# Neighbourhood attention in strips of 16 rows by 8 columns, in a one-core diffusion trunk step

## The chip, the cores and the metric

The kernel runs on one core of one Trainium2 chip. The metric is device microseconds from start to end of one execution; the median of several executions counts. All arithmetic is in 32-bit floats. TensorE (PE) multiplies, VectorE (DVE), ScalarE (ACT) and GpSimd (POOL) do the elementwise work, and all data transfers are issued from SyncE's queue (SP).

## The reference, cut to what matters

One layer of a trunk works on 1024 latent tokens (a grid of 16 rows by 64 columns) and 256 context tokens, each 1024 wide: SwiGLU, then four mixers side by side (A to D, 256 channels each), an output projection, and a second SwiGLU. Mixer C, with 4 heads of 64, is the one that matters here. A latent query sees a window of 8 rows by 16 columns of its grid, clamped at the edges, with a learned bias per offset, and besides all 256 cached context keys, in one softmax:

```python
rs = jnp.clip(rows - wr // 2, 0, R - wr)             # wr = 8, R = 16
row_idx = rs[:, None] + jnp.arange(wr)[None, :]
cs = jnp.clip(cols - NAT_WC // 2, 0, GRID_W - NAT_WC)  # NAT_WC = 16, GRID_W = 64
in_win = (cols[None, :] >= cs[:, None]) & (cols[None, :] < cs[:, None] + NAT_WC)
s_loc = jnp.where(in_win, einsum(q, k[row_idx]) * scale + bias, NEG_INF)
s_ctx = einsum(q, k_ctx) * scale
p = softmax(concatenate([s_loc, s_ctx]))
o = p_loc @ v[row_idx] + p_ctx @ v_ctx
```

## The kernel before, in words

The program is written down in a natural order and recorded by a planner (`Plan`, lines 213 to 413). The planner finds what each instruction needs from earlier ones, and issues them as a list schedule: each engine takes, of the instructions whose inputs are there by the planner's prices (`price`, line 425), the one written first. Nearly every instruction is therefore issued from line 395, and groups in the profile are told apart by tile names. To decide what overlaps, `View.box` (line 139) takes the smallest range that holds a view; for a tensor in DRAM that is a range of addresses from its first to its last element.

The order of the stages is: first SwiGLU, projections and mixers A and D, projection of B, then attention. Attention runs over units, each a tile of 128 queries of one pair of heads: 16 units of mixer B on all latent keys (`Gqa`), 4 of B's context, then for each of the two head pairs of C eight `Nat` units (line 1441) and two `Ctx` units. While unit n's second half (`back`) is written down, unit n+1's first half (`front`) and the query load of unit n+2 (`prep`, `load_q`, line 1222) precede it. Probabilities have 4 buffers, that is two units.

A `Nat` unit holds two grid rows by 64 columns of queries (128). Its keys are all columns of 8 or 9 grid rows (`KR0`, line 28; `nrow` is 9 for units 2 to 5): 512 or 576 local keys, and 256 context keys. For each of two heads, `front` multiplies queries and keys in two products each (the query's high and low part): 512 columns, 64 more where there are 9 rows, 256 context columns. DVE adds the bias and takes the maximum (`tensor_tensor_reduce`, lines 1471 to 1475), ACT takes the exponentials with their sums, and `softmax_tail` (line 1305) multiplies by the reciprocal of the sum; for the second head that is done on POOL where n is 832. `back` calls `pv` (line 1251): TensorE transposes the probabilities in blocks of 128 keys (6 blocks, and one of 64), the first four are copied to SBUF by ACT, the rest by DVE, and each is multiplied with its values; then `split` writes the result as a high part (ACT) and a low part (DVE) into `yh` and `yl`, the input of the output projection.

The projections of C (`c_tasks`, line 1140) are worked by token tile. They store normalised queries and keys (512 columns, `craw`) and values (256, `cvraw`) into a DRAM tensor `csc` [10 tiles, 128 tokens, 768], one transfer for each; the first three tiles before attention, the other tiles as side work between units of B. `CSet` (line 1349) then loads a head pair's keys (`load_k`), values and the bias tables (`bint` 576 columns, `bedge` 896 columns per head). Side work during C is loading the second pair's set, splitting the other mixers' outputs (`y_piece`), and a part of the output projection (`wo_early`, tile `fb`) from unit 5 of the second pair on, which has lower priority and fills TensorE.

Of the kernel before, what the change touches and what calls it, by code (L numbers as in the profile page):

```python
# [27 lines left out]
KR0 = [0, 0, 0, 2, 4, 6, 8, 8]  # L28
# [26 lines left out]
class View:  # L55
    """a part of a planned tile: offset and (size, stride) per dimension, and how to take it from the tile"""
# [156 lines left out]
class Plan:  # L213
# [28 lines left out]
    def record(self, eng, real, meth, a, k):  # L242
# [44 lines left out]
    # -- the list schedule, and the issue in its order --  # L287
# [137 lines left out]
def price(eng, meth, a, k):  # L425
    """about how long an engine is held, in microseconds"""
# [48 lines left out]
def write_down(plan, I, O):  # L475
# [85 lines left out]
    def mod_section_dve(s, f):  # L561
        """128 columns of section s: sum over the features on VectorE"""
# [18 lines left out]
    def mod_tile(ws):  # L581
        """silu(c) times two [1024, 128] tiles of weights: [128 columns, tile, vector]"""
# [14 lines left out]
    def mod_first(f):  # L597
        """128 columns of the first shift and scale"""
# [74 lines left out]
    def gemm_fm(ps, whi, wlo, hh, hl, c, ks=range(KT), first=0, last=KT - 1):  # L673
        """feature-major: ps[128, chunk] = w[:, 128 cols]^T h"""
# [89 lines left out]
    def first(c, fetch, wab, js):  # L764
        """the first block: its products follow the loads of the modulation's weights"""
# [55 lines left out]
    def tables():  # L821
# [17 lines left out]
        # retention tables  # L839
# [37 lines left out]
    # ================= mixers =================  # L877
# [137 lines left out]
    def d_process(p):  # L1015
        """heads 2p and 2p + 1: states of both directions, block-diagonal over the heads; then the tiles' outputs"""
# [122 lines left out]

    def c_tasks(bank, early):  # L1140
        """the projections of C by token tile, for an accumulator of one bank"""
        wts = []

        def qk_tile(t):
# [9 lines left out]
            dma(csc[t][:, 0:512], raw)  # L1154
# [3 lines left out]
        def v_tile(t):  # L1158
# [7 lines left out]
            dma(csc[t][:, 512:768], raw[:, 0:256])  # L1166
# [41 lines left out]
    # ================= attention =================  # L1208
# [13 lines left out]
    def load_q(src, t, pr):  # L1222
        """token-major heads 2pr, 2pr+1 -> [128, 2, 2, 128]: [hi; lo] and [lo; hi] per head"""
# [20 lines left out]
    def PYB(w):  # L1244
        """w columns of the outputs' bank; its groups come one after another"""
        if pyo[0] + w > 512:
            pyo[0] = 0
        pyo[0] += w
        return pyb[:, pyo[0] - w:pyo[0]]

    def pv(pr, t, probs, vtiles):
        """probs[e]: [128 q, nkeys]; vtiles(e): list of (key offset, n keys, v ap [n, 64])"""
        c, o = tok_chunk(t)
# [28 lines left out]
        split(yh[c][:, fi, o:o + P], yl[c][:, fi, o:o + P], py)  # L1282
# [22 lines left out]
    def softmax_tail(probs, sums, n):  # L1305
# [3 lines left out]
        for e in range(2):  # L1309
            (G if e and n == 832 else V).tensor_scalar(probs[e][:, :n], probs[e][:, :n], rs[:, e:e + 1], None, ALU.mult)  # L1310
# [4 lines left out]
    def load_k(src, col, lat, cxt, t0, n, wide=False):  # L1315
        """keys of token tiles, token-major [128, 2 heads, 64] -> [hi; lo] x 128 tokens per tile and head"""
# [33 lines left out]
    class CSet:  # L1350
        """a head pair of C: keys, values and bias"""

        def __init__(self, pr, q):
# [5 lines left out]
            self.bint = q.tile([P, 2, 576], F32, name="bint")  # L1359
            self.bedge = q.tile([P, 2, 896], F32, name="bedge")  # L1360
# [18 lines left out]
    class Ctx:  # L1379
        """context queries on context keys"""  # L1380
# [60 lines left out]
    class Nat:  # L1441
        def __init__(self, pr, i):
            self.pr, self.i = pr, i
            self.kr0 = KR0[i]
            self.nrow = 9 if 2 <= i <= 5 else 8
# [4 lines left out]
        def front(self):  # L1450
            pr, i, qT, kr0, nrow = self.pr, self.i, self.qT, self.kr0, self.nrow
            s_ = sets[pr]
            nk = 64 * nrow
            n = nk + 256
            probs = self.probs = new_probs()
            mx = ap.tile([P, 2, 3], F32, name="mx", tag="mx")
            nm = ap.tile([P, 2], F32, name="nmc", tag="nmc")
            sums = ap.tile([P, 2, 2], F32, name="sums3", tag="sums3")
            r9 = nk - 512
            for e in range(2):  # L1460
                sa, sb = PS2(), PS2()
                qk(sa, qT, e, s_.k[e][:, kr0 * 64:kr0 * 64 + 512])
# [310 lines left out]
```

## Time and profile before

| | us |
|---|---|
| median of 3 runs | 2652.24 |
| fastest, slowest run | 2649.84, 2653.35 |
| span of the profiled execution, first to last instruction | 2647.6 |
| TensorE busy | 2604.6 |
| VectorE, ScalarE, GpSimd busy | 1338.2, 740.4, 199.4 |
| TensorE's share of the chain that ended last | 93% |

The page gives the profiled execution by its span only, with no time of its own beside it; the span is 4.6 us below the median of the runs. Busy time is a union of the instructions of an engine; TensorE's matmuls are pipelined and their ends are modelled, so its busy time counts the tails of its products as busy. The chain of waits takes each instruction from where the one before it on the chain ended, and so shows what TensorE spends per product when products follow one another.

### The profile page before, as it was taken

To read this page: it belongs to the slowest core of one execution; us is meant where nothing else is said; L and a number is where in the kernel's file an instruction comes from. 1 tells how busy PE (TensorE), PEld (TensorE's weight loads), DVE (VectorE), ACT (ScalarE), POOL (GpSimd) and SP (SyncE) were. 2 spreads that over 40 slices of the span, in tenths; PEclk is the share of its full clock that TensorE was granted. 3 is DMA by queue.
4 is the path that set the end of the run, shared out by engine and by line. 5 is a ranking of instruction groups with operands and counts; after the bars stand their busy time and mean duration, and the time that the engine had idled before them with its cause. 6 is when DMAs were issued, how large, how long until landed. Compare 5 with 4: busy or idle time off the path is not lost.

```text
span 2647.6 us, 36536 instructions
## 1 busy us (share of the span) xinstructions
PE 2604.6 (98%) x14960; PEld 2192.8 (83%) x14960; DVE 1338.2 (51%) x2653; ACT 740.4 (28%) x1417; POOL 199.4 (8%) x243
## 2 busy tenths in 40 slices
PE   7999999999999999999999999999999999999999
PEld 5888888888888878887778678888888888888888
DVE  6755666554342374477665784354343233433433
ACT  5211111111111165322674783341111111111111
POOL 0000000000000041122100251220000000000000
PEclk9999999999999999999999999999999999999999
DMA  8322222222011131341301423011111111110112
GB/s 298 111 87 84 92 84 78 94 80 64 33 32 48 33 113 66 112 126 57 101 29 41 139 76 120 25 44 53 33 40 40 33 48 32 40 41 32 48 33 88
DMA packets 92119, 187.12 MB, mean 71 GB/s; under 512 B 9904, under 2 KB 39600, under 8 KB 91824
## 3 DMA queue, kind: packets, MB, share of 16 engines
q1 hardware_dynamic: 91952, 184.80, 21.1%
q8 instruction: 117, 1.92, 0.3%
q14 instruction: 50, 0.41, 0.0%
HBM read 156.97 MB, written 27.79 MB: 70 GB/s over the span
## 4 chain that ended last, share of the span: by engine, by line
PE 93%; DVE 5%; ACT 1%; issue 1%; DMA 1%; SPq 0%; POOL 0%; ACTq 0%; DVEq 0%; POOLq 0%
PE po L395 23%; PE pa L395 22%; PE pb L395 22%; PE pgd L395 3%; PE fb L395 3%; PE ptb L395 3%; PE pwo L395 3%; PE pyb L395 3%; PE ps L395 3%; PE p L395 1%; PE pd L395 1%; DVE nt L395 1%; DVE hl L395 1%; DVE dst L395 1%; PE pgate L395 1%; PE dpa L395 1%
## 5 line engine op out<-in xcount | busy, mean ns | idle before, releaser
L395 PE MATMUL po<-uh,whi 128*128 128x512 f32 (+1 forms) x1056 | 376.3, 356 | 4.3 <-DVE x L395 4.3
L395 PE MATMUL po<-ul,whi 128*128 128x512 f32 (+1 forms) x1056 | 375.7, 356 | 0.0
L395 PE MATMUL po<-uh,wlo 128*128 128x512 f32 (+1 forms) x1056 | 375.4, 356 | 0.0
L395 ACT CAST whi<-raw 128x1024 fp32r<-128x1024 f32 x162 | 168.5, 1049 | 715.7 <-PE po L395 487.7
L395 PE MATMUL pa<-hh,whi 128*128 128x512 f32 (+1 forms) x1024 | 363.5, 355 | 0.0
L395 PE MATMUL pb<-hh,whi 128*128 128x512 f32 (+1 forms) x1024 | 362.9, 354 | 0.0
L395 PE MATMUL pa<-hh,wlo 128*128 128x512 f32 (+1 forms) x1024 | 361.7, 353 | 0.0
L395 PE MATMUL pb<-hh,wlo 128*128 128x512 f32 (+1 forms) x1024 | 361.6, 353 | 0.0
L395 PE MATMUL pa<-hl,whi 128*128 128x512 f32 (+1 forms) x1024 | 359.9, 351 | 0.1
L395 PE MATMUL pb<-hl,whi 128*128 128x512 f32 (+1 forms) x1024 | 359.6, 351 | 0.0
L395 DVE TENSOR_TENSOR silu<-silu,pb 128x256 f32<-128x256 f32 (+1 forms) x128 | 76.2, 596 | 522.1 <-PE pb L395 522.1
L395 DVE TENSOR_TENSOR wlo<-raw,whi 128x1024 fp32r<-128x1024 f32 x162 | 198.3, 1229 | 181.4 <-ACT whi L395 179.1
L395 DVE SCALAR_TENSOR_TENSOR xr<-po,modT,xr 128x512 f32<-128x512 f32 (+1 forms) x264 | 174.1, 662 | 110.9 <-PE po L395 110.7
L395 PEld LDWEIGHTS po<-uh,whi 128*128 128x128 f32 x1056 | 198.6, 188 | 37.6 <-DVE x L395 5.1
L395 PEld LDWEIGHTS po<-ul,whi 128*128 128x128 f32 x1056 | 198.8, 188 | 32.5
L395 PEld LDWEIGHTS po<-uh,wlo 128*128 128x128 f32 x1056 | 198.7, 188 | 32.5
L395 PEld LDWEIGHTS pa<-hh,wlo 128*128 128x128 f32 x1024 | 192.1, 188 | 29.5
L395 PEld LDWEIGHTS pb<-hh,wlo 128*128 128x128 f32 x1024 | 192.0, 187 | 29.5
L395 PEld LDWEIGHTS pa<-hl,whi 128*128 128x128 f32 x1024 | 192.2, 188 | 28.6 <-DVE hl L395 0.5
L395 PEld LDWEIGHTS pb<-hl,whi 128*128 128x128 f32 x1024 | 192.2, 188 | 28.3 <-issue 0.2
L395 PEld LDWEIGHTS pa<-hh,whi 128*128 128x128 f32 x1024 | 192.4, 188 | 26.0 <-issue 0.4
L395 ACT CAST uh<-silu 128x512 fp32r<-128x512 f32 x132 | 72.2, 548 | 506.8 <-DVE silu L395 506.8
(446 smaller groups left out, 3969.7 us busy)
## 6 DMA issues: line engine op xcount, KB each, us to landing
raw<-in_w SPq DMA_DIRECT2D x132, 512.0 KB, 3.6
wh<-in_wmodT SPq DMA_DIRECT2D x96, 256.0 KB, 2.6
wmt<-in_wmod SPq DMA_DIRECT2D x20, 512.0 KB, 6.9
raw<-in_wfm SPq DMA_DIRECT2D x10, 512.0 KB, 3.5
xr<-xs SPq DMA_DIRECT2D x8, 640.0 KB, 6.5
x<-in_xT SPq DMA_DIRECT2D x16, 256.0 KB, 5.5
xs<-x SPq DMA_DIRECT2D x16, 256.0 KB, 2.0
raw<-in_wo SPq DMA_DIRECT2D x8, 512.0 KB, 3.5
```

The source lines that it names most:

```text
L395: getattr(real, meth)(*[f(v) for v in a], **{q: f(v) for q, v in k.items()})
```

## The change

Units of C are cut from the grid in the other direction. A `Nat` unit is now a strip of all 16 grid rows by 8 columns (128 queries again, so 8 units per head pair), and its keys are its own strip and the one on either side: 384 local keys for units 1 to 6, 256 for units 0 and 7. The window's rows are now part of the mask, which the host writes into the bias tables. The tokens are put into strip order when the projections are stored to `csc`, by two transfers of 64 tokens per tile in place of one; results go back to token order in `pv`, by two strided splits of 64 columns. The context scores of both heads share one bank (`PS1`) and one maximum; the second head's multiplication goes to POOL where n is 640.

```diff
+    def to_strips(t, col, src):
+        n = src.shape[1]
+        if t >= 8:
+            dma(csc[t][:, col:col + n], src)
+            return
+        for rr in range(2):
+            r = 2 * t + rr
+            dma(csc[0:8, 8 * r:8 * r + 8, col:col + n], src[64 * rr:64 * rr + 64])
...
-            dma(csc[t][:, 0:512], raw)
+            to_strips(t, 0, raw)
...
-            dma(csc[t][:, 512:768], raw[:, 0:256])
+            to_strips(t, 512, raw[:, 0:256])
...
     def pv(pr, t, probs, vtiles):
...
-        split(yh[c][:, fi, o:o + P], yl[c][:, fi, o:o + P], py)
+        if t >= 8:
+            c, o = tok_chunk(t)
+            split(yh[c][:, fi, o:o + P], yl[c][:, fi, o:o + P], py)
+            return
+        for c in range(2):
+            h, l = (y[c][:, fi, :].rearrange("p (r w) -> p r w", w=64)[:, :, 8 * t:8 * t + 8] for y in (yh, yl))
+            split(h, l, py[:, 64 * c:64 * c + 64].rearrange("p (r w) -> p r w", w=8))
...
-            (G if e and n == 832 else V).tensor_scalar(probs[e][:, :n], probs[e][:, :n], rs[:, e:e + 1], None, ALU.mult)
+            (G if e and n == 640 else V).tensor_scalar(probs[e][:, :n], probs[e][:, :n], rs[:, e:e + 1], None, ALU.mult)
...
-            self.bint = q.tile([P, 2, 576], F32, name="bint")
-            self.bedge = q.tile([P, 2, 896], F32, name="bedge")
+            self.bint = q.tile([P, 2, 384], F32, name="bint")
+            self.bedge = q.tile([P, 2, 512], F32, name="bedge")
...
     class Nat:
         def __init__(self, pr, i):
             self.pr, self.i = pr, i
-            self.kr0 = KR0[i]
-            self.nrow = 9 if 2 <= i <= 5 else 8
+            self.t0 = max(i - 1, 0)
+            self.nt = 3 if 0 < i < 7 else 2
...
         def front(self):
...
+            s1 = PS1()
             for e in range(2):
-                sa, sb = PS2(), PS2()
-                qk(sa, qT, e, s_.k[e][:, kr0 * 64:kr0 * 64 + 512])
-                if r9:
-                    qk(sb[:, 0:r9], qT, e, s_.k[e][:, kr0 * 64 + 512:kr0 * 64 + nk])
-                qk(sb[:, r9:r9 + 256], qT, e, s_.k[e][:, NLAT:T])
...
+                qk(s1[:, e], qT, e, s_.k[e][:, NLAT:T])
+            V.tensor_reduce(mx[:, :, 1], s1, AX.X, ALU.max)
+            for e in range(2):
+                sa = PS2()
+                qk(sa[:, :nk], qT, e, s_.k[e][:, self.t0 * P:self.t0 * P + nk])
+                bias = s_.bint[:, e] if self.nt == 3 else s_.bedge[:, e, 0:256] if self.i == 0 else s_.bedge[:, e, 256:512]
+                V.tensor_tensor_reduce(probs[e][:, 0:nk], sa[:, :nk], bias, 1.0, -3.0e38, ALU.add, ALU.max,
                                        mx[:, e, 0:1])
...
+                V.tensor_reduce(nm[:, e:e + 1], mx[:, e], AX.X, ALU.max, negate=True)
+                S.activation(probs[e][:, nk:n], s1[:, e], AF.Exp, bias=nm[:, e:e + 1], accum_out=sums[:, e, 1:2])
                 S.activation(probs[e][:, 0:nk], probs[e][:, 0:nk], AF.Exp, bias=nm[:, e:e + 1],
                              accum_out=sums[:, e, 0:1])
...
+                out = [(r * P, P, s_.v[:, (t0 + r) * P + 64 * e:(t0 + r) * P + 64 * e + 64]) for r in range(nt)]
+                return out + [((nt + a) * P, P, s_.vc[:, a, 64 * e:64 * e + 64]) for a in range(2)]
```

## Rows read from the trace of the kernel before

**Rows 1.** The page's first part: busy time of each engine.

```profile
PE 2604.6 (98%) x14960; PEld 2192.8 (83%) x14960; DVE 1338.2 (51%) x2653; ACT 740.4 (28%) x1417; POOL 199.4 (8%) x243
```

**Rows 2.** Windows: start:end, length, busy time of each engine, clock, DMA share, GB/s.

```profile
1500.00:1560.00 60.00, 56.55 (x505) 45.05 (x504) 48.55 (x170) 48.88 (x139) 29.74 (x43) 1.00 0.37 112
...
1560.00:1580.00 20.00, 19.86 (x157) 15.23 (x156) 16.31 (x62) 18.23 (x53) 9.64 (x17) 1.00 0.32 94
...
1560.00:1596.00 36.00, 35.48 (x288) 27.98 (x287) 29.72 (x108) 29.65 (x81) 19.13 (x27) 1.00 0.27 86
...
1596.00:1621.60 25.60, 25.60 (x227) 20.12 (x225) 16.26 (x53) 15.74 (x47) 3.66 (x4) 1.00 0.15 43
```

**Rows 3.** The chain of waits, 1500 to 1621.6 us: shares by line.

```profile
by line: PE ptb L395 26.3%; PE pyb L395 25.2%; PE ps L395 23.6%; PE fb L395 6.9%; DVE prob L395 5.8%; ACT prob L395 2.9%; issue 1.9%; DVE wlo L395 1.4%; DVE rsm L395 1.0%; DVE ckT L395 0.9%; DVE kd L395 0.9%; DVE pT L395 0.8%; ACT whi L395 
```

**Rows 4.** The chain of waits, pieces in C: start us, us, what, count.

```profile
1517.23 1.45 PE pyb L395 x22
...
1537.72 0.47 PE ps L395 x2
...
1542.77 0.76 PE ptb L395 x7
...
1545.77 0.36 PE pyb L395 x2
...
1546.57 1.82 PE pyb L395 x26
...
1601.51 1.16 PE ps L395 x6
```

**Rows 5.** Groups on ACT, 1500 to 1621.6 us: shapes, count, busy us, mean ns, idle.

```profile
L395 ACT COPY pT<-ptb 128x512 f32<-128x512 f32 x32 | 18.0, 589 | 1.4 <-PE ptb L395 1.3
...
L395 ACT ACTIVATE prob<-ps,nmc 128x256 f32<-128x256 f32 x32 | 15.2, 476 | 5.7 <-DVE nmc L395 5.4
...
L395 ACT ACTIVATE prob<-prob,nmc 128x576 f32<-128x576 f32 x16 | 12.3, 771 | 0.0
...
L395 ACT ACTIVATE prob<-prob,nmc 128x512 f32<-128x512 f32 x16 | 11.6, 722 | 0.0
...
L395 ACT CAST hh<-pyb 128x128 fp32r<-128x128 f32 x20 | 5.3, 263 | 8.5 <-PE pyb L395 8.5
```

**Rows 6.** The same groups on DVE.

```profile
L395 DVE COPY pT<-ptb 128x256 f32<-128x256 f32 x32 | 13.3, 418 | 6.8 <-PE ptb L395 5.1 <-PE pyb L395 1.5
...
L395 DVE TENSOR_SCALAR prob<-prob,rsm 128x768 f32<-128x768 f32 x16 | 9.1, 612 | 0.0
...
L395 DVE TENSOR_SCALAR prob<-prob,rsm 128x832 f32<-128x832 f32 x8 | 7.3, 909 | 0.0
...
L395 DVE COPY pT<-ptb 64x128 f32<-64x128 f32 x16 | 4.3, 271 | 0.0
...
L395 DVE CUSTOM_DVE_ANT_0 prob<-ps,bint 128x64 f32<-128x64 f32 x16 | 3.4, 210 | 1.1 <-PE ps L395 1.1
```

**Rows 7.** Instructions in order of time, POOL and DVE, one interior unit.

```profile
1538.90 2.36 POOL L395 TENSOR_SCALAR prob<-prob,rsm 128x832 f32<-128x832 f32 x1 [1.78 <-DVE rsm L395]
...
1539.22 1.08 DVE L395 TENSOR_SCALAR prob<-prob,rsm 128x832 f32<-128x832 f32 x1
```

**Rows 8.** Windows of 5 us: columns as in rows 2.

```profile
1475.00:1480.00 5.00, 3.02 (x19) 2.38 (x21) 4.75 (x7) 1.94 (x6) 2.60 (x2) 0.72 0.19 52
...
1550.00:1555.00 5.00, 4.00 (x44) 3.31 (x42) 4.23 (x11) 4.58 (x13) 2.83 (x6) 1.00 0.20 65
```

**Rows 9.** DMA issues, 1240 to 1621.5 us: count, KB each, us to landing.

```profile
csc<-craw SPq DMA_DIRECT2D x10, 256.0 KB, 2.0
```

**Rows 10.** SP's queue in order of time, and the instructions on tile kd.

```profile
1438.38 0.42 SPq L395 DMA_DIRECT2D kr<-csc  x1
...
1441.28 0.32 SPq L395 DMA_DIRECT2D csc<-cvraw  x1
...
L395 ACT CAST kd<-kr x12: 299/412/437, 1462.5 to 1521.2; 128x256 fp32r<-128x256 f32 x8, 128x128 fp32r<-128x128 f32 x4
```

More of the change, by code (lines that the diff above doesn't have):

```diff
@@ L27 @@
 CO = NLAT + 3
-KR0 = [0, 0, 0, 2, 4, 6, 8, 8]
 SM_FIELDS = [
@@ L1251, in pv @@
     def pv(pr, t, probs, vtiles):
-        c, o = tok_chunk(t)
         py = PYB(P)
@@ L1450, in front @@
         def front(self):
-            pr, i, qT, kr0, nrow = self.pr, self.i, self.qT, self.kr0, self.nrow
-            s_ = sets[pr]
-            nk = 64 * nrow
+            qT, s_ = self.qT, sets[self.pr]
+            nk = P * self.nt
             n = nk + 256
             probs = self.probs = new_probs()
-            mx = ap.tile([P, 2, 3], F32, name="mx", tag="mx")
+            mx = ap.tile([P, 2, 2], F32, name="mx", tag="mx")
             nm = ap.tile([P, 2], F32, name="nmc", tag="nmc")
             sums = ap.tile([P, 2, 2], F32, name="sums3", tag="sums3")
-            r9 = nk - 512
+            s1 = PS1()
@@ L1478, in front @@
-                S.activation(probs[e][:, nk:n], sb[:, r9:r9 + 256], AF.Exp, bias=nm[:, e:e + 1],
-                             accum_out=sums[:, e, 1:2])
+                qk(s1[:, e], qT, e, s_.k[e][:, NLAT:T])
[5 more added lines that the diff above has]
+                V.tensor_tensor_reduce(probs[e][:, 0:nk], sa[:, :nk], bias, 1.0, -3.0e38, ALU.add, ALU.max,
+                                       mx[:, e, 0:1])
+                V.tensor_reduce(nm[:, e:e + 1], mx[:, e], AX.X, ALU.max, negate=True)
+                S.activation(probs[e][:, nk:n], s1[:, e], AF.Exp, bias=nm[:, e:e + 1], accum_out=sums[:, e, 1:2])
@@ L1484, in back @@
         def back(self):
-            s_, kr0, nrow, pr = sets[self.pr], self.kr0, self.nrow, self.pr
-            nk = 64 * nrow
+            s_, t0, nt = sets[self.pr], self.t0, self.nt
             def vt(e):
-                out = []
-                for r in range(0, nrow - 1, 2):
-                    tt_ = (kr0 + r) // 2
-                    out.append((r * 64, P, s_.v[:, tt_ * P + 64 * e:tt_ * P + 64 * e + 64]))
-                for a in range(2):
-                    out.append((nk + a * P, P, s_.vc[:, a, 64 * e:64 * e + 64]))
-                if nrow == 9:
-                    tt_ = (kr0 + 8) // 2
-                    out.append((512, 64, s_.v[:64, tt_ * P + 64 * e:tt_ * P + 64 * e + 64]))
-                return out
-            pv(pr, self.i, self.probs, vt)
+                out = [(r * P, P, s_.v[:, (t0 + r) * P + 64 * e:(t0 + r) * P + 64 * e + 64]) for r in range(nt)]
+                return out + [((nt + a) * P, P, s_.vc[:, a, 64 * e:64 * e + 64]) for a in range(2)]
+            pv(self.pr, self.i, self.probs, vt)
     dma(bvr[:, 0:10], bsc[:, :, 384:512].rearrange("t p e -> p t e"))
@@ L1719, in _pack, with strip @@
     out["cvc"] = C(a["cache_c_v"][0, 0].reshape(2, P, 256).transpose(1, 0, 2))
-    q, k = r(64)[:, None], r(64)[None, :]
-    cs = np.clip(q - 8, 0, 48)
-    inw = (k >= cs) & (k < cs + 16)
-    dc = np.clip(k - q + 15, 0, 30)
     tab = a["nat_bias"][0]
-    full = np.where(inw[None, None], tab[:, :, dc], f(-1e30)).astype(f)
-    neg = np.full((4, 64, 64), -1e30, f)
-    def blk(jt, jb):
-        top = full[:, jt] if jt is not None else neg
-        bot = full[:, jb] if jb is not None else neg
-        return np.concatenate([top, bot], axis=1)
-    out["bedge"] = C(np.concatenate([blk(jj, jj - 1) for jj in range(1, 15)], axis=2))
-    out["bint"] = C(np.concatenate([blk(jj if jj < 11 else None, jj - 1 if jj > 3 else None)
-                                    for jj in range(3, 12)], axis=2))
+    rr, cc = r(P) // 8, r(P) % 8
+    rs = np.clip(rr - 4, 0, 8)
+    def strip(i, strips):
+        q = 8 * i + cc
+        cs = np.clip(q - 8, 0, 48)
+        kr = np.concatenate([rr for _ in strips])
+        kc = np.concatenate([8 * t + cc for t in strips])
+        inw = (kc[None] >= cs[:, None]) & (kc[None] < cs[:, None] + 16)
+        inw &= (kr[None] >= rs[:, None]) & (kr[None] < rs[:, None] + 8)
+        dr = np.clip(kr[None] - rr[:, None] + 7, 0, 14)
+        dc = np.clip(kc[None] - q[:, None] + 15, 0, 30)
+        return np.where(inw[None], tab[:, dr, dc], f(-1e30)).astype(f)
+    out["bedge"] = C(np.concatenate([strip(0, (0, 1)), strip(7, (6, 7))], axis=2))
+    out["bint"] = C(strip(3, (2, 3, 4)))
     return out
```

11 lines of the change are left out of this document (removed).

## The prediction

> **What bounds the kernel now.** The busy times come first: TensorE is busy for 98% of the span, the others for about half or less [rows 1]. But that is a mean over stages, and the change touches only one, the units of mixer C, so windows come second. Between 1500 and 1621.6 us, TensorE, VectorE and ScalarE are all busy: of 121.6 us, 117.6, 94.5 and 94.3 [rows 2]. TensorE's figure counts the tails of its products, so the third view is the chain of waits over the same stretch. TensorE's four tiles hold 26.3 + 25.2 + 23.6 + 6.9 = 82.0% of it, 99.7 us; the other 21.9 us are steps of DVE and ACT for which TensorE waits [rows 3]. So C is bound mostly by TensorE and for the rest by the softmax, with ACT close behind: in the best 20 us ACT is busy for 18.23, 91% [rows 2]. The last 25.6 us are TensorE alone on the chain; the output projection's early part fills its gaps there.
>
> **TensorE's work, step by step.** What a product costs in a row of products is read from the chain [rows 4].
> Scores: two products of 512 columns take 0.47, so 0.235 each; the row of six, 1.16, is two of 512 and four of 64 or 256 columns, and the four then take (1.16 - 0.47) / 4 = 0.17. A product of 384 columns isn't in this trace. It lies between those two, 0.17 and 0.235; I take 0.19, nearer the small ones, since 256 columns already cost no more than 64 (what sets that price is not their number). Unit by unit, two heads, two products each: units 2 to 5 go from 4 x 0.235 + 8 x 0.17 = 2.30 to 4 x 0.19 + 4 x 0.17 = 1.44, a saving of 0.86; units 1 and 6 from 1.62 to 1.44, 0.18; units 0 and 7 from 1.62 to 8 x 0.17 = 1.36, 0.26.
> Transposes: 0.76 for seven, 0.109 each. Units 2 to 5 go from 14 to 10, units 1 and 6 from 12 to 10, units 0 and 7 from 12 to 8: 0.43, 0.22 and 0.43.
> Values: units 2 to 5 take 0.36 + 1.82 = 2.18 for 28 products, edge units 0.36 + 1.45 = 1.81 for 24. With 20 or 16 left, at 1.45 / 22 = 0.066 apiece, that is 1.55 or 1.28: savings of 0.63, 0.26 and 0.53.
> The sums are 1.92, 0.66 and 1.22 us for a unit of the three kinds. Both head pairs have four, two and two of them: 8 x 1.92 + 4 x 0.66 + 4 x 1.22 = 22.9 us off TensorE. With 384 columns at 0.235 it is 20.7, at 0.17 23.9.
>
> **What is late next.** If the other 21.9 us of the chain stayed as they are, C would take 121.6 - 22.9 = 98.7 us. ACT doesn't allow that. Its work hardly falls: an exponential of 576 or 512 columns takes 0.771 or 0.722 [rows 5], 0.0008 per column, so 384 columns about 0.62 and 256 about 0.525; the context's 256 (0.476) stay, and the copies of four transposed blocks (0.589) too. The two splits of 64 columns replace one of 128 at 0.263. Their price isn't shown: by the 128 columns it lies between half of that (0.13 each, nothing added) and all of it (0.26 each); I take 0.21, since 64 columns fewer save 0.05 at 0.0008 each, so +0.16 per unit. ACT's net is -0.14, -0.04 and -0.23 per unit of the three kinds: -2.2 us in all, of some 94.
> Until 1596 ACT is busy for 48.88 + 29.65 = 78.5 of 96 us [rows 2]. About three quarters of its saving falls there, which leaves 76.8. At its best share, 91%, that takes 84.4 us: 11.6 less than now. After 1596 TensorE decides, and of the second pair's units about the last three fall there, one of each kind: 1.92 + 0.66 + 1.22 = 3.8. Together 15.4 us. TensorE's remaining work, 99.7 - 22.9 = 76.8, then fills 72% of a stretch of 106 us: it no longer is the bound.
>
> **DVE** is relieved by more than ACT, so it does not take ACT's place: in units 2 to 5 the copy of 256 columns (0.418) becomes one of 128 (0.27 by the row of that width), that of the 64-key block (0.271) and the bias step of 64 columns (0.210) go, for two heads (0.148 + 0.271 + 0.210) x 2 = 1.26 us a unit [rows 6]; the maximum of both heads in one instruction saves a little more, the second split adds about as much. I count no gain for it beyond letting ACT reach its best share; where the chain's own DVE steps shrink too, that is the first rival.
>
> **POOL's multiplication** moves to 12 units instead of 8. At 640 columns it takes 2.36 x 640 / 832 = 1.82 [rows 7]. In units 1 and 6 it replaces a DVE instruction of 0.612 [rows 6], so the second head's probabilities come about 0.6 later there; a unit lasts over 5 us and another is in flight, which hides it. Without that cover: 4 x 0.6 = 2.4 us. Beside POOL's instruction from 1538.90 to 1541.26, DVE's own multiplication ran from 1539.22 and was over at 1540.30 [rows 7]: slowed (0.909 on average, against 0.612 x 832 / 768 = 0.66 alone [rows 6]), but not kept out.
> [...]
>
> **The stores in strips.** Sixteen transfers (8 tiles of queries and keys, 8 of values) become 32. Their ranges of addresses in `csc` now overlap, so the planner chains each to the one before; a tile's store takes about 2.0 us to land [rows 9], so SP may stand for up to 2 us per half, 4 to 8 us in a unit of B. Behind it in SP's queue stand query loads for two units ahead and stores of B's outputs, which have a unit or more to spare. I cost this at 0, with +4 us if the first tiles' stores delay B's first query loads. The first load of C's keys, issued at 1438.38, can no longer precede the value store of the last latent tile (1441.28); with 4 us of chained halves it is issued at about 1446, and its first user starts at 1462.5 [rows 10]: hidden. Bias tables are smaller, and nobody waits for them. The output projection needs C's last feature tile complete in all latent columns, which it now is only after unit 7; two context units still follow, so nothing waits.
>
> **The sum.** Profiled span 2647.6 - 15.4 = 2632.2; the median of the runs lies 4.6 above that span, so 2636.8, taken as 2637.
>
> **Rivals.**
> First, TensorE's whole term comes through: ACT gets denser than in any row, or the DVE steps on the chain shrink as well. For it: DVE frees over 20 us. Against it: ACT would need 92.1 of 98.7 us, 93%. 2652.2 - 22.9 = 2629.
> Second, ACT paces C at the share it has now. For it: ACT is the engine whose work doesn't fall, and 78.5 / 96 = 82% is what it reached with TensorE and DVE in the way. Against it: those two are what it waited for. Then its 1.7 us become 1.7 / 0.82 = 2.1, and with the 3.8 of the end 5.9 are saved: 2646.
> Third, the context scores now sit in one of the four banks that the transposes share, from the first product to the last exponential. If each unit's transposes wait 1 us for a bank, 16 us go back: 2653, no change. Against it: a filling is four transposes and a copy, 0.44 + 0.589 [rows 4, 5], about 1.2 us with the steps between; five of them a unit on three banks are 2.0 us of over 5.
> [...]
> [...]
>
> **How the numbers follow.** The forecast gets 0.62 (its own range 2631 to 2643), the first rival 0.10, the second 0.18, the third 0.05, the fourth 0.05. The range of 8 in 10 runs from below the first rival's 2629 to beyond the second's 2646: 2628 to 2648. A change of 0.2% is 5.3 us, about what a measurement of this kernel tells from none. Faster by more: 0.62 + 0.10 + 0.11 of the second rival, 0.83; within: 0.07 + 0.05 = 0.12; slower: 0.05.
>
> **What would show it.** After the change, 8 x 4 + 4 x 2 + 4 x 4 = 56 transposes fewer in C, and score products at a pace of 0.17 to 0.19; C shorter by 11 to 20 us; TensorE's share of the chain there well under 82% and ACT's well above; ACT near 90% busy. Stretches outside C the same to 2 us. I would be wrong on the mechanism if C shrank by less than 6 us with ACT under 85%, if SP's waits for a store of `csc` stood ahead of TensorE on the chain, or if the granted clock in C fell.

## The result, and the profile after

| | before | after |
|---|---|---|
| median of 4 runs each, us | 2651.04 (2649.69 to 2653.35) | 2637.49 (2635.66 to 2639.83) |
| ratio, with its 95% interval | | 0.9946 [0.9932, 0.996] |
| span of the profiled execution, us | 2647.6 | 2638.0 |

The changed kernel is 13.6 us faster in the medians, where 15.4 were forecast. That 2637 itself was met to half a microsecond is luck in part: the kernel before has a median of 2651.0 here, 1.2 below the one that the forecast started from. The 4.6 us that the forecast put between span and median do not hold for the changed kernel either: its profiled execution was the slowest of the four, 2639.83, and its span lies 0.5 us above their median. The span of the profiled execution falls by 9.6 us only, so the two executions are first cut into stages. B begins with the first score product on its keys, C with the first on tile `ckT`, and the output projection with the first product into tile `pwo`.

| | B begins | C begins | projection begins | B to C | length of C | after C |
|---|---|---|---|---|---|---|
| before | 1284.5 | 1500.2 | 1621.4 | 215.7 | 121.2 | 1026.2 |
| after | 1289.4 | 1505.1 | 1615.0 | 215.7 | 109.9 | 1023.0 |

C is 11.3 us shorter and what follows it 3.2, together 14.5. The 4.9 us ahead of B go the other way, and they come in steps: held against the kernel before, TensorE's instructions stand 1.5 us later from 50 us on, 2.0 from 1000, 3.7 from 1250, and 4.9 at the start of B. Three of the four steps lie at falls of the granted clock that the profile before doesn't have (columns as in [rows 2]; before, all three windows have 1.00):

```profile
20.00:30.00 10.00, 8.26 (x108) 5.53 (x105) 6.21 (x16) 3.77 (x9) 0.00 (x0) 0.83 0.99 377
1220.00:1225.00 5.00, 5.00 (x29) 4.88 (x30) 2.71 (x19) 0.37 (x1) 1.27 (x1) 0.66 0.18 66
1285.00:1290.00 5.00, 4.82 (x25) 4.03 (x26) 3.11 (x7) 3.00 (x7) 2.10 (x6) 0.66 0.25 79
```

In windows of 1 us the lower clock is 0.50 (1222 to 1224, 1287 to 1289), half of full speed. By the shares of the granted clock TensorE was at half speed for 17.1 us ahead of B in this execution, and for 6.8 in the one before; at half a microsecond for each, an estimate from the 0.50, the difference is worth 5.1 us at the most. Of the change itself only the first tiles' stores in strips lie there, issued from 1278.0 on. In plain_stores below, which has none, B begins at 1285.1, and in the other eleven experiments between 1283.9 and 1288.0. So these 4.9 us are mostly the clock of one execution; but in after_again too, the changed kernel once more, B begins 3.4 us later than before (1287.9), so a lasting shift of a microsecond or two can't be excluded.

The page's first part, to be held against [rows 1]: TensorE loses 16.2 us of busy time, ACT 4.8, DVE 18.9, POOL gains 3.7.

```profile
PE 2588.4 (98%) x14760; PEld 2182.0 (83%) x14760; DVE 1319.3 (50%) x2593; ACT 735.6 (28%) x1433; POOL 203.1 (8%) x247
```

Windows of the changed kernel, with the columns of [rows 2]: all of C, its first 96 us, its densest 20, and four of 5 us.

```profile
1505.10:1615.00 109.90, 100.94 (x839) 82.13 (x837) 75.11 (x270) 89.15 (x280) 57.13 (x77) 0.97 0.33 98
...
1505.10:1601.10 96.00, 87.07 (x719) 70.89 (x717) 68.03 (x244) 80.92 (x251) 57.13 (x77) 0.96 0.36 107
...
1560.00:1580.00 20.00, 19.10 (x147) 15.09 (x145) 15.33 (x57) 18.43 (x58) 13.35 (x21) 1.00 0.40 107
...
1520.00:1525.00 5.00, 2.32 (x28) 1.97 (x28) 2.86 (x9) 4.44 (x16) 2.21 (x1) 1.00 0.38 122
1525.00:1530.00 5.00, 5.00 (x32) 4.51 (x31) 4.20 (x13) 3.46 (x8) 3.21 (x5) 0.66 0.55 157
1535.00:1540.00 5.00, 3.69 (x32) 3.00 (x32) 3.71 (x15) 4.22 (x14) 4.21 (x5) 0.86 0.17 52
1540.00:1545.00 5.00, 4.91 (x42) 4.27 (x40) 2.76 (x11) 4.05 (x13) 2.97 (x5) 0.80 0.23 69
```

ACT is busy for 84% of the first 96 us (80.92) and for 81% of C, where it had 82% of the first 96 us before [rows 2]; it reaches 92% only in the best 20 us. DVE fell from four fifths of C to two thirds (75.11 of 109.90). And TensorE's granted clock was at its lower level for part of 1525 to 1530 and of 1535 to 1545, as it never was in this stretch before (1.00 in all four windows of [rows 2]). In windows of 1 us it is 0.50 from 1525 to 1528 and from 1539 to 1542. By the shares, 0.66, 0.86 and 0.80 of 5 us each, that is 6.8 us of C at half speed, which by the same estimate cost 3.4 us at the most. A row of products takes longer at it: five transposes of probabilities took 1.33 us at 0.50, and five others 0.71 at 1.00 (start us, us, what).

```profile
1540.48 1.33 PE L394 MATMUL ptb<-ident,prob 128*128 128x128 f32 x5
...
1542.50 0.71 PE L394 MATMUL ptb<-ident,prob 128*128 128x128 f32 x5
```

The chain of waits over C by lines (it answers to [rows 3]), and pieces of it (to [rows 4]):

```profile
by line: PE pyb L394 22.3%; PE ptb L394 22.2%; PE ps L394 15.4%; PE fb L394 12.2%; ACT prob L394 9.9%; issue 3.6%; ACT pT L394 2.4%; DVE prob L394 2.0%; DVE mx L394 1.8%; DVE ckT L394 1.4%; DVE kd L394 1.2%; DVE pT L394 1.0%; ACT hh L394 0.
...
1582.79 0.70 PE ps L394 x4
...
1593.10 0.47 PE ps L394 x4
...
1593.91 1.24 PE pyb L394 x18
```

TensorE's four tiles hold 72.1% of 109.9 us, 79.2, where they held 99.7. ACT's exponentials (`ACT prob`) went from 2.9% to 9.9%, from 3.5 to 10.9 us. So C is no longer bound by one engine alone: TensorE still paces most of it, and waits for the softmax in the rest.

The groups of C on ACT and DVE, and POOL's multiplication (1504 to 1615 us; columns as in [rows 5]):

```profile
L394 POOL TENSOR_SCALAR prob<-prob,rsm 128x640 f32<-128x640 f32 x12 | 25.3, 2111 | 22.4 <-ACT pT L394 10.2 <-DVE hl L394 7.4 <-DVE rsm L394 3.5
...
L394 ACT COPY pT<-ptb 128x512 f32<-128x512 f32 x32 | 18.1, 601 | 2.7 <-PE ptb L394 2.5
...
L394 ACT ACTIVATE prob<-prob,nmc 128x384 f32<-128x384 f32 x24 | 14.9, 621 | 0.0
...
L394 DVE TENSOR_SCALAR prob<-prob,rsm 128x640 f32<-128x640 f32 x12 | 6.9, 573 | 0.3
...
L394 ACT CAST hh<-pyb 128x64 fp32r<-128x64 f32 x32 | 5.2, 218 | 2.1 <-PE pyb L394 2.1
...
L394 ACT ACTIVATE prob<-prob,nmc 128x256 f32<-128x256 f32 x8 | 4.1, 509 | 0.0
```

### The profile page after: what moved, and what is told of

The parts are those of the page before. It is cut to its first block, busy times and chain, and to the rows that moved or that the text cites. A ratio compares the mean times of both kernels' runs of the same rounds, so it can differ in the third digit from the quotient of the medians.

```text
span 2638.0 us, 36134 instructions
## 1 busy us (share of the span) xinstructions
PE 2588.4 (98%) x14760; PEld 2182.0 (83%) x14760; DVE 1319.3 (50%) x2593; ACT 735.6 (28%) x1433; POOL 203.1 (8%) x247
## 4 chain that ended last, share of the span: by engine, by line
PE 92%; DVE 5%; ACT 2%; issue 1%; DMA 1%; POOL 0%; SPq 0%; ACTq 0%; POOLq 0%; DVEq 0%
PE po L394 23%; PE pa L394 22%; PE pb L394 22%; PE fb L394 3%; PE pgd L394 3%; PE pwo L394 3%; PE ptb L394 3%; PE pyb L394 2%; PE ps L394 2%; PE p L394 1%; PE pd L394 1%; DVE nt L394 1%; PE dpa L394 1%; DVE dst L394 1%; PE pgate L394 1%
```

## The experiments

Each is an edit of the changed kernel. Ratios are to the kernel before, on the same chip; those of one group share its runs. The changed kernel itself, run again with the first group, gives the measure for all: 2639.83 us, 0.9951 [0.9938, 0.9963], C 109.9 us.

| | median us | ratio [95%] | length of C |
|---|---|---|---|
| after_again | 2639.83 | 0.9951 [0.9938, 0.9963] | 109.9 |
| act_less | 2639.31 | 0.9949 [0.9937, 0.9962] | 110.4 |
| pe_back | 2648.25 | 0.9983 [0.9974, 0.9992] | 117.3 |
| plain_stores | 2639.84 | 0.9950 [0.9936, 0.9963] | 109.8 |
| no_pool | 2642.82 | 0.9964 [0.9952, 0.9976] | 115.5 |
| packed | 2635.47 | 0.9935 [0.9923, 0.9947] | 107.8 |
| deep | 2636.54 | 0.9939 [0.9928, 0.9951] | 110.8 |
| late_keys | 2634.61 | 0.9932 [0.9920, 0.9943] | 106.7 |
| act_more | 2644.88 | 0.9967 [0.9954, 0.9979] | 117.6 |
| dve_more | 2642.43 | 0.9954 [0.9941, 0.9968] | 114.8 |
| act_skip | 2632.85 | 0.9922 [0.9910, 0.9935] | 104.5 |
| best | 2633.66 | 0.9922 [0.9910, 0.9934] | 104.8 |

> The changed kernel once more, to see how much of it is the execution's own spread. Its profiled execution had C (first score product of C to first product of the output projection) at 109.9 us against 121.2, mixer B's stretch (first score product of B to first of C) at 215.7 against 215.8, and the start of B 4.9 us later. Theory: the 4.9 us ahead of B are the spread of an execution (start-up, two short falls of the granted clock), so here the start of B lies within 3 us of the kernel before and the ratio is 0.993 to 0.996. Rival: the stores in strips or another order of issue cost them, and the start of B is again 4 to 6 us late.

It came out as the first profile had it, C to a tenth of a microsecond. The start of B was 1287.9 instead of 1289.4, 3.4 us later than before: between the 3 us of the theory and the 4 to 6 of the rival, so it settles neither. The mean granted clock of the execution was 0.995, as in the first profile (0.997 before).

**act_less: half of ACT's copies of transposed blocks go to DVE.**

```diff
-                    eng = V.tensor_copy if g0 == 4 else S.copy
+                    eng = V.tensor_copy if g0 == 4 or (e and nv > 2) else S.copy
```

> In the strip units the copies of four transposed blocks of the second head go from ACT (0.60 us each, 16 of them, 9.6 us) to DVE, which takes about 0.69 for as many columns and was busy for 75 of 110 us. Theory (ACT paces C where TensorE stalls): C is 4 to 8 us shorter than 109.9, the time about 2632, ratio 0.991 to 0.993. Rival (TensorE still sets C, or the wait from step to step whatever the engine): C within 2 us of 109.9, 2637.

The windows over C and over all of B, and the chain over C, of this kernel:

```profile
1503.80:1614.20 110.40, 100.24 (x837) 79.96 (x836) 85.52 (x285) 82.11 (x264) 56.01 (x77) 1.00 0.33 98
...
1284.10:1503.80 219.70, 212.71 (x1687) 172.96 (x1685) 131.31 (x258) 147.71 (x363) 27.62 (x65) 0.97 0.16 47
```

```profile
by line: PE ptb L394 18.9%; PE pyb L394 15.5%; PE ps L394 13.4%; PE fb L394 10.8%; DVE prob L394 8.6%; issue 8.2%; ACT prob L394 7.6%; DVE mx L394 3.9%; DVE pT L394 2.1%; DVE ckT L394 1.7%; DVE kd L394 1.6%; DVE hl L394 1.5%; DVE nmc L394 1
```

A miss: ACT lost 7.0 us of busy time and C gained 0.5, although the clock stayed at full speed here. But DVE gained 10.4, and its steps came onto the chain in ACT's place (`DVE prob` from 2.0% to 8.6%). This run exchanged one load for another, so it neither shows nor refutes that ACT sets the pace; that took single loads, in the last group. One thing more is seen here: in B, four windows of 5 us between 1465 and 1490 had granted clocks of 0.52 to 0.80, and B took 219.7 us instead of 215.7. By the shares that is 13.7 us of B at half speed, 10.3 more than in the changed kernel, and B is 4.0 us longer, 0.39 for each. So in B, where TensorE decides (busy for 212.71 of the 219.70 us), the lower clock was paid in the time.

**pe_back: TensorE's saving is given back, by multiplying the values twice in every strip unit.**

```diff
-        for i in range(nv):
+        for i in [*range(nv)] * (2 if nv > 2 else 1):
```

> Every strip unit multiplies its transposed probabilities with the values twice, one pass after the other, same result: 12 x 20 + 4 x 16 = 304 more products of 0.066 us, 20 us of work given back to TensorE and nothing to the others. Theory (TensorE no longer sets most of C): C longer by 6 to 13 us, since only the parts where TensorE is dense pay in full, 2644 to 2650. Rival (TensorE still bounds C): 18 to 20 us longer, 2656.

```profile
1501.00:1618.30 117.30, 112.58 (x1119) 92.87 (x1118) 74.92 (x267) 89.98 (x280) 57.05 (x77) 1.00 0.30 88
```

Twelve units have 20 products more and four have 16, 304 in all; at 0.061 (the pace of the doubled rows here, shown at the end) to 0.069 (1.24 / 18 in the changed kernel) that is 18.5 to 21.0 us, taken as 20. C took 7.4 us more and what follows it 2.5 (1025.5 against 1023.0): 9.9, half of what was given. So half of the work given to TensorE in C fits into gaps where it waits for others.

**plain_stores: the tokens are stored in their old order, one transfer a tile; C then attends to other tokens.**

```diff
-        if t >= 8:
+        if True:
             dma(csc[t][:, col:col + n], src)
```

> The stores of C's projections in token order, one transfer per tile as before the change: the regrouping into strips is left out, so C attends to other tokens than it should. Theory (stores cost nothing): within 2 us of the changed kernel, B's stretch at 215 to 216, first load of C's keys back to about 6 us earlier with no effect on C's start. Rival: B's stretch or its start 3 to 5 us shorter, 2633.

C took 109.8 us and B 215.8, and the median is that of after_again: the strip stores cost nothing that these runs can tell. What they do in SP's queue is seen in the changed kernel, the stores of values late in B's stretch (start us, us, what):

```profile
1442.20 0.58 SPq L394 DMA_DIRECT2D csc<-cvraw  x1
...
1443.74 3.80 SPq L394 DMA_DIRECT2D csc<-cvraw  x3
1447.59 0.44 SPq L394 DMA_DIRECT2D kr<-csc  x1
```

The halves are chained as forecast (4 us for three), and the key load comes at 1447.59 (forecast 1446, before 1438.38 [rows 10]). Nothing on the chain waits for it.

**no_pool: the second head's multiplication goes back to DVE.**

```diff
-            (G if e and n == 640 else V).tensor_scalar(probs[e][:, :n], ...
+            V.tensor_scalar(probs[e][:, :n], probs[e][:, :n], rs[:, e:e + 1], None, ALU.mult)
```

> The second head's multiplication by the reciprocal of its sum stays on VectorE in all strip units, where the changed kernel has it on GpSimd in 12 of them (2.1 us each there, about 0.5 on VectorE). VectorE gets about 6 us more work in C, and a unit's second head is ready some 1.5 us sooner. Theory (C is paced by the steps of a unit from engine to engine, with two units in flight, and by no engine's load): C 3 to 8 us shorter than 109.9, time 2630 to 2635. Rival (it is VectorE's and ScalarE's load together): C as long or 2 to 3 us longer, 2638 to 2641.

The window over C, and DVE's group:

```profile
1504.20:1619.70 115.50, 102.37 (x837) 81.29 (x835) 82.64 (x281) 89.19 (x280) 34.79 (x65) 0.97 0.32 93
```

```profile
L394 DVE TENSOR_SCALAR prob<-prob,rsm 128x640 f32<-128x640 f32 x24 | 13.8, 616 | 0.2
```

A miss, and a useful one: 7.5 us more on DVE made C 5.6 us longer, where the theory had it shorter and the rival 3 us longer at the most, with the clock no lower than in the changed kernel. POOL takes over three times as long for the same tile (2.11 us against 0.62), and the twelve multiplications are still better placed there; without them on POOL, half of the 11.3 us in C would be gone. It also shows that DVE, at two thirds of C, is not free.

**packed, deep: more units in flight.** `packed` puts both heads' probabilities into one buffer, which makes four units' worth instead of two; `deep` has besides a third buffer for queries and writes unit n+2's first half ahead of unit n's second.

```diff
-            probs = self.probs = new_probs()
+            pk = ap.tile([P, T], F32, name="prob", tag="prob", bufs=4)
+            probs = self.probs = [pk[:, 0:640], pk[:, 640:1280]]
...
-        if n + 1 < len(units):
+        if n >= nB - 1 and n + 2 < len(units):
+            units[n + 2].front()
```

> Both heads' probabilities of a strip unit (640 columns at most each) share one buffer of 1280 columns, so that the same four buffers hold four units instead of two; the order in which the work is written stays. Theory (two units in flight pace C, by their probability buffers): C 4 to 10 us shorter than 109.9. Rival (what keeps a third unit from starting is the order of issue and the transposes' banks, or the buffers were never waited for: the changed kernel's waits show 2.1 us in 4 times for them): C within 2 us.

> As the one before, and in C the first half of unit n+2 is written down ahead of the second half of unit n (n+1 in the changed kernel), the query load one unit earlier, with three buffers for queries instead of two. Theory (a unit's steps from engine to engine pace C): 6 to 15 us off C's 109.9, time 2624 to 2632. Rival (each engine's load, or the four banks of which two are then held by context scores): C within 3 us of 109.9 or longer.

```profile
1501.20:1609.00 107.80, 100.03 (x838) 80.89 (x837) 75.88 (x269) 88.90 (x280) 57.15 (x77) 0.98 0.34 100
```

```profile
1505.00:1615.80 110.80, 104.14 (x837) 81.69 (x835) 73.59 (x269) 88.68 (x280) 57.96 (x74) 0.97 0.33 96
```

C is 2.1 us shorter with `packed`, of which up to 1.7 can be the clock (3.4 us of C at the lower level instead of 6.8), and 0.9 longer with `deep`; neither median differs from the changed kernel's by more than the intervals allow. The chain over C in `deep` shows why that is not the whole story:

```profile
by line: PE pyb L394 26.1%; PE ptb L394 25.1%; PE ps L394 18.6%; PE fb L394 10.9%; ACT prob L394 6.0%; issue 3.6%; DVE prob L394 2.2%; ACT pT L394 1.7%; DVE mx L394 1.2%; ACT hh L394 1.1%; DVE kd L394 0.9%; DVE hl L394 0.7%; ACT qT L394 0.4
```

The steps of the other engines and issue fell from 30.7 to 21.4 us of the chain, and TensorE's four tiles rose from 79.2 to 89.4 in exchange. So more units in flight did shorten the waits between engines, but not C, and the theory that these waits alone hold C up is out. Whether TensorE's added time comes from the banks that the context scores of two units then hold, as the expectation has it, was not tried.

**late_keys: the second pair's keys are loaded six side tasks later.** This follows a reading of the changed kernel: in 1520 to 1525 TensorE was busy for 2.32 of 5 us (above). Here are instructions in order of time there, on TensorE and then on DVE and ACT (in brackets: idle before, and what ended it):

```profile
1520.59 0.70 PE L394 MATMUL pyb<-pT,cvc 128*64 128x128 f32 x7
1523.57 0.54 PE L394 MATMUL ptb<-identr,kd 128*128 128x128 f32 x4 [2.27 <-DVE kd L394]
```

```profile
1522.08 0.16 DVE L394 TENSOR_REDUCE rsm<-sums 128x2 f32<-128x4 f32 x1 [2.41 <-ACT prob L394]
...
1522.63 0.55 DVE L394 TENSOR_SCALAR prob<-prob,rsm 128x640 f32<-128x640 f32 x1
1523.10 1.27 DVE L394 TENSOR_TENSOR kd<-kr,kd 128x256 fp32r<-128x256 f32 x2
...
1522.13 0.74 ACT L394 CAST kd<-kr 128x256 fp32r<-128x256 f32 x2
```

TensorE's next instruction is the transposition of the second pair's keys. It needs their low part from DVE, and DVE stands in its own order behind a sum of exponentials that ACT delivers at 1522.08. DVE could not have begun much sooner in any case: the low part needs the high part from ACT, and ACT came to that at 1522.13, behind the same exponentials. So both queues hold the keys up. The lower clock of 1525 to 1530 (0.66 in these 5 us) comes right behind this wait.

```diff
-            side = sets[1].tasks() + ys
+            side = ys[:6] + sets[1].tasks() + ys[6:]
```

> The second head pair's keys, values and bias are loaded after the first six of the other mixers' outputs rather than ahead of them, some four units later. In the changed kernel TensorE waited 2.3 us for those keys' low parts at 1521 to 1524, and the granted clock fell to 0.66 of full speed in the 5 us after it, and again at 1540. Theory (the wait and the fall that follows it cost C about 4 us together): C 106 to 108 and no half clock in it. Rival (the wait only moves to where the keys are then split): C within 1.5 us of 109.9 with a fall elsewhere.

```profile
1500.90:1607.60 106.70, 98.54 (x837) 79.24 (x835) 76.46 (x268) 88.41 (x280) 57.49 (x77) 1.00 0.34 101
...
1520.00:1525.00 5.00, 4.84 (x50) 4.01 (x46) 4.01 (x18) 4.54 (x16) 4.50 (x4) 1.00 0.26 66
1540.00:1545.00 5.00, 3.31 (x34) 2.56 (x33) 3.58 (x9) 4.62 (x15) 3.84 (x6) 1.00 0.33 103
```

The wait is gone (TensorE is busy for 4.84 of the 5 us), the clock stays at full speed throughout C, and C is 3.2 us shorter. How much of that is the wait and how much the clock, this run does not separate: the 6.8 us at the lower clock that are gone are worth up to 3.4. The median is not told apart from the changed kernel's; that C is shorter rests on one profile, against 109.9, 109.9 and 109.8 us in the changed kernel's two and in plain_stores.

**act_more, dve_more, act_skip: one load at a time.** Behind each head's maximum, ACT copies 512 columns that nobody reads (`act_more`, 0.63 us each), or DVE reduces them (`dve_more`, 0.68 us each); `act_skip` leaves out one of ACT's copies of four blocks per strip unit (its bank then waits for no copy, and one buffer `ph` less is in use per unit). The three edits in one cut, with comments added:

```diff
-                V.tensor_reduce(nm[:, e:e + 1], mx[:, e], AX.X, ALU.max, negate=True)
+                at = V.tensor_reduce(nm[:, e:e + 1], mx[:, e], AX.X, ALU.max, negate=True)
+                plan.after = at
+                junk = ap.tile([P, 512], F32, name="junk", tag="junk", bufs=1)
+                S.copy(junk, s_.bedge[:, e])     # dve_more: a V.tensor_reduce into [P, 1]
+                plan.after = None
...
+                if e and g0 == 0 and nv > 2:     # act_skip, in pv
+                    pts[e].append(pts[0][0])
+                    continue
```

> Each strip unit has two more copies of 512 columns on ACT, from the bias table to a buffer that nobody reads, placed after the maxima; about 0.53 us each, 32 of them, 17 us, and nothing for the other engines. Theory now (C is set by ACT and DVE together with the order of issue, each added microsecond of ACT costing more than half; the copies moved from ACT to DVE earlier brought nothing because DVE took up more than ACT lost): C 9 to 17 us longer than 109.9. Rival (ACT's load decides nothing, the steps from engine to engine do): under 5 us longer.

> The same on DVE: two more maxima over 512 columns of the bias table per strip unit, about 0.6 us each, 32 of them, 19 us, read by nobody. DVE was busy for 75 of 110 us. Theory: DVE has room, but taking work to it cost 5.6 us for 7.5 when GpSimd's multiplication was moved there, so 8 to 14 us longer. Rival (only ACT and TensorE matter): under 4 us longer.

> The copy of the second head's first four transposed blocks is left out in the strip units (the second head's values are weighted with the first head's probabilities there): 16 x 0.60 = 9.6 us off ACT, nothing put on another engine. Theory (ACT's load is one of the two that count): C 5 to 9 us shorter than 109.9. Rival (ACT's load decides nothing): within 2 us.

The windows over C, of act_more, of dve_more and of act_skip:

```profile
1502.70:1620.30 117.60, 102.30 (x837) 81.95 (x835) 76.66 (x269) 104.48 (x312) 56.81 (x77) 0.97 0.31 92
```

```profile
1505.00:1619.80 114.80, 104.09 (x837) 83.12 (x835) 91.75 (x301) 89.79 (x280) 55.63 (x77) 0.96 0.31 95
```

```profile
1505.80:1610.30 104.50, 96.98 (x833) 78.96 (x832) 74.06 (x268) 81.87 (x264) 56.41 (x77) 0.98 0.33 101
```

| | busy time of the engine in C | length of C | per us | spent at the lower clock in C |
|---|---|---|---|---|
| act_more | ACT +15.3 | +7.7 | 0.50 | 6.8 (changed kernel 6.8) |
| dve_more | DVE +16.6 | +4.9 | 0.30 | 10.2 |
| no_pool | DVE +7.5, POOL -22.3 | +5.6 | 0.75 | 6.8 |
| act_skip | ACT -7.3 | -5.4 | 0.74 | 3.4 |
| pe_back | TensorE +20 | +7.4 | 0.37 | 0 |

The last column is worked out from the granted clock in windows of 5 us. A microsecond at the lower clock costs half of one at the most by the estimate from its 0.50 (in B it cost 0.39), so dve_more's rate lies between 3.2 / 16.6 = 0.19 and 0.30, act_skip's between 3.7 / 7.3 = 0.51 and 0.74, and pe_back's between 0.37 and 10.8 / 20 = 0.54. act_skip came out as its theory had it; act_more and dve_more came out between theory and rival, each load counting, but for less than expected. No engine's microsecond is worth a whole one, and none is worth nothing. In that sense C is held by several engines together. By these rates act_less nearly cancels: 7.0 us off ACT at 0.50 give 3.5, and 10.4 on DVE at 0.30 take 3.1 of them. But it had C at full clock, which should have given up to 3.4 us more and did not show, so that part is open. Nor do the runs separate how much an engine has to do from where the added step stands: act_more's copies stand ahead of the exponentials in every unit. What the rates don't explain is no_pool, whose 7.5 us on DVE cost more than twice dve_more's rate. There the multiplication is itself a step that the transposes wait for, while dve_more's reduction sits ahead of the exponentials; that this is the reason was not tried.

**best: late_keys and packed together.**

> The later loads of the second head pair and the shared probability buffer, both together: 3.2 and 2.1 us shorter C by themselves. If they are two different waits, C is 104 to 105 and the time about 2632; if the shared buffer only covers the same wait for the second pair's keys, C is 106 to 107 and the time as with the later loads alone, 2634.6.

```profile
1503.50:1608.30 104.80, 97.00 (x838) 79.31 (x836) 75.97 (x269) 88.52 (x280) 56.37 (x77) 1.00 0.34 102
```

C takes 104.8 us, 5.1 less than in the changed kernel, at full clock, with ACT busy for 84% of all of it. At 0.9922 [0.9910, 0.9934] it is faster than the kernel before. Against the changed kernel it is 0.2 to 0.3% ahead: the interval ends just below that of after_again (from 0.9938) and touches that of the first timing (from 0.9932). From late_keys alone it is not told apart.

## Why the prediction was right

| part of the sum, us | forecast | measured |
|---|---|---|
| TensorE's attention tiles on the chain of C | -22.9 | -25.5 |
| early output projection (`fb`) on the chain of C | 0 | +5.0 |
| steps of the other engines, and issue, on the chain of C | +7.5 | +8.8 |
| what follows C | 0 | -3.2 |
| C and what follows | -15.4 | -14.5 |

The forecast's second and third terms are those of its own sum: C of 121.6 - 15.4 = 106.2 us, less 76.8 of TensorE, leaves 29.4 for the others, 7.5 more than their 21.9. The measured ones are shares of the chain times its length, 121.6 us before [rows 3] and 109.9 after; by these C shortens by 11.7, by the stages by 11.3, at the lower edge of the 11 to 20 that the prediction named as its sign. TensorE's share fell to 72% as said; ACT near 90% busy did not come.

**TensorE's work.** The 56 transposes are gone, 560 before and 504 now by the group on the probabilities:

```profile
L395 PE MATMUL ptb<-ident,prob x560: 270/273/476, 1298.2 to 1618.7; 128*128 128x128 f32 x182, 128*64 128x128 f32 x5
...
L394 PE MATMUL ptb<-ident,prob x504: 270/273/476, 1303.1 to 1612.6; 128*128 128x128 f32 x168
```

Paces: a product of 384 columns takes 0.70 / 4 = 0.174 (forecast 0.19), one of 256 takes 0.47 / 4 = 0.118 (forecast 0.17). By tile the chain lost 11.8 us of scores (forecast 8.6), 7.6 of transposes (6.1) and 6.1 of values (8.2). The forecast read its row of six score products [rows 4] wrongly. By shapes, that row holds four of 512 columns and two of 256, and none of 64:

```profile
L395 PE MATMUL ps<-ckT,qT 128*128 128x512 f32 x4 | 1.3, 414 | 0.0
L395 PE MATMUL ps<-ckT,qT 128*128 128x256 f32 x2 | 0.4, 282 | 0.0
```

So 4 x 0.235 + 2 x 0.118 = 1.18 make up its 1.16, and 0.17 is the price of no product. One of 64 columns takes 0.11: in 14 pairs of them in the kernel before, the second ends that long behind the first. On the chain, one such second:

```profile
1531.94 0.11 PE ps L395
```

With these prices the units of the three kinds save 0.69, 0.24 and 0.47 us, and 8 x 0.69 + 4 x 0.24 + 4 x 0.47 = 8.4, nearly the 8.6 forecast: the price of the small products was too high before and after alike, and in the sum the errors nearly cancelled, which is luck. What the chain lost beyond that are products that left it: 27 of the 48 of 384 columns still stand on it, and the other 21 at 0.174 are 3.7 us. The reason given for the 384 columns, that the number of columns doesn't set the price of the small products, holds between 64 and 256 columns (0.11 and 0.118) and not above (0.174 and 0.235 for 384 and 512).

**"ACT doesn't allow that."** In size right, in the mechanism half. That something keeps a third of TensorE's saving is so: the others' steps on the chain grew by 8.8 us, ACT's exponentials alone by 7.4. But ACT does not run at 91%: it has 84% of the first 96 us and 81% of C. The forecast made one engine the new bound and took its best share; the rates above show ACT, DVE and TensorE to share it, at 0.5 to 0.7 per microsecond of ACT, 0.2 to 0.3 of DVE (more in no_pool) and 0.4 to 0.5 of TensorE. ACT's own load was mis-sized too: its busy time in C fell by about 5 us, not 2.2. The exponentials came as priced (0.621 and 0.509 us against 0.62 and 0.525), the splits also (0.218 against 0.21), but the splits follow one another closely and overlap: 32 of them occupy 5.2 us, 0.16 each, and so added 1.0 us where the forecast had 2.6. With 89.15 us of work, 91% would have given C 98 us. Two errors of this step, a load too high and a share too high, offset each other.

**The end.** The 3.8 us after 1596 were expected inside C; they came partly behind it. The early part of the output projection, which fills TensorE's gaps, began its last product at 1649.2 before, 28 us into the projection; now TensorE has gaps enough, and all of it lies in C:

```profile
L395 PE MATMUL fb<-hh,wlo x21: 280/388/475, 1576.6 to 1649.2; 128*128 128x512 f32 x14, 128*128 128x256 f32 x7
...
L394 PE MATMUL fb<-hh,wlo x21: 279/393/467, 1571.1 to 1614.7; 128*128 128x512 f32 x14, 128*128 128x256 f32 x7
```

That is the +5.0 in C and the -3.2 behind it: before, 26 of its 63 products stood behind C, 3.6 us of the chain, now none, and in pe_back 23 again. "Stretches outside C the same to 2 us" was wrong for this one.

**DVE and POOL.** "I count no gain for it beyond letting ACT reach its best share": no_pool and dve_more show that DVE's relief counts by itself. POOL's instruction takes 2.11 us on average, not 1.82, and it stands nowhere on the chain over C, so its delay is hidden, as costed. What the two instructions cost beside one another went here with which of them started first. In nine of the twelve units DVE's multiplication of the first head had started 0.13 to 0.18 us ahead; it then took its usual 0.55, and POOL's took 2.13 to 2.40. In the other three POOL's took 1.89; DVE's took 0.80 where it started 0.34 behind POOL's, and 0.54 where it started 0.61 behind. One unit of each kind, POOL's instruction and then DVE's:

```profile
1537.88 2.17 POOL L394 TENSOR_SCALAR prob<-prob,rsm 128x640 f32<-128x640 f32 x1 [0.23 <-ACT pT L394]
...
1537.74 0.55 DVE L394 TENSOR_SCALAR prob<-prob,rsm 128x640 f32<-128x640 f32 x1
...
1588.29 1.89 POOL L394 TENSOR_SCALAR prob<-prob,rsm 128x640 f32<-128x640 f32 x1 [1.32 <-DVE nmc L394]
...
1588.63 0.80 DVE L394 TENSOR_SCALAR prob<-prob,rsm 128x640 f32<-128x640 f32 x1
```

The kernel before has the same: four of DVE's multiplications of 832 columns started 0.07 to 0.37 us behind POOL's and took 1.05 to 1.33, the other four 0.64 to 0.65. So in these traces the one that starts closely behind the other takes longer, but not to the other's end: DVE's 0.80 were over 0.75 us before POOL's 1.89. The prediction's "slowed" stands, and what DVE loses in the changed kernel is far from the whole of POOL's instruction: 0.25 us in one of the twelve units.

**The rivals.** ACT at its present share (5.9 us saved) is out, but not by the number: its share did stay near 82%, and with the measured load this rival gives 89.15 / 0.82 = 108.7 us, close to C. It is out by act_more, where 15.3 us more on ACT would then have added 18.7 and added 7.7. The whole TensorE term is out: 14.5 of 22.9, or of 25.5. The bank for the context scores is out too: ahead of the transposes of probabilities in C, TensorE sat idle for 1.0 us in all, where 1 us for each of 16 units was the rival's price:

```profile
L394 PE MATMUL ptb<-ident,prob 128*128 128x128 f32 x180 | 29.4, 288 | 1.0 <-DVE pT L394 0.8
```

The fourth, a slower kernel at 0.05, is out: no run shows one, and what the runs show of a slower clock is at most 10.2 us of C at half speed (dve_more). In the changed kernel that came in miniature, 6.8 us of C, at 3.4 us at the most; the prediction named a fall of the granted clock in C as a sign against itself, and it may have taken a share of what was gained. What brings a fall was not shown. The first one in C came behind a wait of 2.27 us, and the kernel before had 0.72 from 1475 to 1480, where TensorE was busy for 3.02 of 5 us [rows 8]; but it kept 1.00 at 4.00 of 5 us [rows 8], and so did 1540 to 1545 in late_keys, at 3.31 of 5 us.

## What to carry to other kernels

When a saving on the bound engine leaves several engines at some 70 to 90% in the same stretch, as here, it may be that no one of them sets the new time; give each a rate by adding a known load to it alone, and price the next edit by the sum over engines, as a first estimate only: here it missed no_pool by more than a factor of two. The exchange of work between ACT and DVE gave nothing (C 110.4 against 109.9); giving work to POOL, which is off the path, gave 5.6 us of C even at three times the duration (2.11 us against 0.62). And look first at what stands ahead of what in each engine's order: a load moved by six side tasks was worth 3 us of C together with the clock fall that went with it, where leaving out a twelfth of ACT's work gave 5. When a price is read from a row of products, look first at the shapes of the row.

## What the runs showed of the hardware that was not expected

- A score product's price is nearly the same for 64 and 256 columns and rises with their number from there: 0.11, 0.118, 0.174 and 0.235 us for 64, 256, 384 and 512.
- Of the multiplications of 640 columns on DVE and POOL, the one that starts closely behind the other takes longer: 0.80 instead of 0.55 us on DVE (started 0.34 behind), 2.13 to 2.40 instead of 1.89 on POOL (0.13 to 0.18 behind).
- A store of half a tile's values into strips takes SP 0.58 us to issue, against 0.32 for a whole one before [rows 10].
- Of value products given twice, 38 in a row take 2.33 us in pe_back, 0.061 apiece, against 0.069 in rows of 18:

```profile
1550.32 2.33 PE pyb L394 x38
```
